# Every second column as the stationary operand: two feature tiles interleaved in each 256 columns of a weight unit

## The chip, the cores and the metric

The program runs on one core of a Trainium2 chip, batch 1, sequence 256, model width 1024. The metric is the device time of one execution in microseconds (us), as the median of several runs. Per-instruction times are in nanoseconds (ns).

## The reference

Two transformer blocks follow one another on the same 256 tokens. The first normalises its input, projects it with one wide matrix, runs two attention mixers (one with a learnt index that keeps the top 64 keys, one with compressed, selected and windowed keys), gates and adds their outputs, and ends in a squared-ReLU feed-forward layer. The second has a gated feed-forward layer, a mixer of dilated-window attention and an mLSTM, and a second gated feed-forward layer. What counts here is that nearly all of the work is products of the 256 tokens with float32 weight matrices:

```python
h = rmsnorm(x, norm_mix[l])
proj = h @ w_in[l]
...
x = x + jnp.square(jax.nn.relu(h @ w_mlp_in[l])) @ w_mlp_out[l]
...
f = swiglu(rmsnorm_2(x, ffn1_pre_g[l]), ffn1_w_gate[l], ffn1_w_up[l], ffn1_w_down[l])
x = x + 0.5 * rmsnorm_2(f, ffn1_post_g[l])
```

## The kernel before, in words

Every weight matrix is an object of class `Wt` (L40). It cuts the columns into chunks, mostly 512 wide (`widths`), and the rows into tiles of 128; a **unit** is two row tiles of one chunk, 128 x 1024 numbers, 512 KB. `layout` (L56) writes the units one after another into the array that the kernel receives; this happens on the host before the run and is outside the time. `plan` (L206) lists all 364 units in the order in which they are used.

For each unit `stream_dma` (L225) issues one DMA on SyncE's queue into a tile `raw`, and `stream_split` (L237) makes two tiles of it: ScalarE rounds `raw` to float32r as `hi` (L251), VectorE writes the remainder `lo = raw - hi` (L252). Both read and write whole rows, left to right. The activations are split in the same manner into `xh` and `xl`. A product then takes three matmuls: hi with xh, hi with xl, lo with xh. `load_unit` (L257) keeps splits two units ahead and DMAs five units ahead.

There are two ways to use a unit:

- `gemm_feat` (L322): the weights are the **stationary** operand. A block of 128 columns ("feature tile" f, four to a 512-wide chunk) is loaded into TensorE, and the 256 tokens stream past as the moving operand; the result has features on the partitions. For each row tile k and each f it issues the three matmuls L334, L336, L337, and each of them comes with its own weight load. Two feature tiles share one PSUM bank. 5,448 matmuls of the run are of this kind (1,816 on each line). All are 128 wide but 8 on each line, the 96 columns at the end of the first chunk of `W_IN1`.
- `gemm_tok` (L276): the tokens are stationary, two tiles of 128, and the weight columns stream past (L290 to L292), 512, 386 or 352 at a time.

Which chunk goes which way is written out in the code: the out- and down-projections (`W_OUT1`, `W_MO`, `W_D1`, `W_OUT2`, `W_D2`), chunk 4 of `W_IN1` and chunks 6 to 9 and 14 to 17 of `W_IN2` go through `gemm_tok`, everything else through `gemm_feat`.

TensorE's instructions stand in the order in which the program and its scheduler wrote them; smaller jobs (attention, transposes) are put in between by `flush` after each row tile. SyncE's and GpSimd's orders are those of the code.

The stationary operand is cut out of `hi` and `lo` like this:

```python
for f in range(nf):
    fs = slice(f * 128, min(f * 128 + 128, w))
    o = ps[f // 2][:fs.stop - fs.start, f % 2, :]
    nc.tensor.matmul(o, hi[:, fs], xh[:, k, :], start=(k == 0 and f % 2 == 0), stop=False,
                     skip_group_check=True)
```

Of the kernel before, what the change touches and what calls it, by code (L numbers as in the profile page):

```python
# [21 lines left out]
D = 1024  # L22
# [6 lines left out]
FF2 = 2816  # L29
VIF = 386  # L30
# [5 lines left out]
def widths_of(n):  # L36
    return [512] * (n // 512) + ([n % 512] if n % 512 else [])


class Wt:  # L40


    def __init__(self, name, k, widths):
        self.name, self.k, self.widths = name, k, widths
        self.kt = k // 128
        self.off, o = [], 0
        for w in widths:
            row = []
            for u in range(0, self.kt, KT):
                n = min(KT, self.kt - u)  # L50
                row.append((o, u, n))
                o += 128 * n * w
            self.off.append(row)
        self.size = o

    def layout(self, w):  # L56
        out = np.empty(self.size, w.dtype)
        c0 = 0
        for c, wd in enumerate(self.widths):
            for o, u, n in self.off[c]:  # L60
                blk = w[u * 128:(u + n) * 128, c0:c0 + wd].reshape(n, 128, wd).transpose(1, 0, 2)
                out[o:o + 128 * n * wd] = blk.reshape(-1)
            c0 += wd
        return out


def win1_columns():
    o = {}
    p = 0
    for n, w in (("q_a", 512), ("k_a", 64), ("v_a", 64), ("q_i", 256), ("k_i", 32), ("w_i", 8), ("q_b", 512),  # L70
                 ("kc", 128), ("vc", 128), ("ks", 128), ("vs", 128), ("kw", 128), ("vw", 128), ("g_b", 24),
                 ("g_br", 2048)):
        o[n] = np.arange(p, p + w)
        p += w
    qb = o["q_b"].reshape(2, 4, 64).transpose(1, 0, 2).reshape(-1)
    cols = [o["q_i"], o["k_a"], o["k_i"],
            o["kc"], o["vc"], o["ks"], o["kw"],
            o["q_a"], qb,
            o["v_a"], o["vs"], o["vw"], o["w_i"], o["g_b"],
            o["g_br"]]  # L80
    return np.concatenate(cols)


def win2_columns():
    o = {}
    p = 0
    for n, w in (("q", 1536), ("k", 1536), ("v", 1536), ("qk", 2048), ("v_m", 1024), ("o_m", 1024), ("if", 8),
                 ("g_a", 1024), ("g_m", 1024)):
        o[n] = np.arange(p, p + w)
        p += w  # L90
    cols = []
    for g in range(3):
        cols += [o["q"][g * 512:(g + 1) * 512], o["k"][g * 512:(g + 1) * 512]]
    cols += [o["v"], o["if"], o["qk"], o["v_m"], o["o_m"], o["g_a"], o["g_m"]]
    return np.concatenate(cols)


W_IN1 = Wt("w_in", D, [352] + [512] * 3 + [352] + [512] * 4)
W_BRA = Wt("w_branch_a", 512, [512] * 2)
W_BRB = Wt("w_branch_b", 512, [512] * 2)  # L100
W_OUT1 = Wt("w_out", D, [512] * 2)
W_MI = Wt("w_mlp_in", D, [512] * 8)
W_MO = Wt("w_mlp_out", 4096, [512] * 2)
FFW = widths_of(FF2)
W_G1 = Wt("ffn1_w_gate_2", D, FFW)
W_U1 = Wt("ffn1_w_up_2", D, FFW)
W_D1 = Wt("ffn1_w_down_2", FF2, [512] * 2)
W_IN2 = Wt("w_in_2", D, [512] * 6 + [VIF] * 4 + [512] * 12)
W_ATT = Wt("w_att_branch_2", 512, [512] * 2)
W_MLB = Wt("w_mlstm_branch_2", D, [512] * 2)  # L110
W_OUT2 = Wt("w_out_2", D, [512] * 2)
W_G2 = Wt("ffn2_w_gate_2", D, FFW)
W_U2 = Wt("ffn2_w_up_2", D, FFW)
W_D2 = Wt("ffn2_w_down_2", FF2, [512] * 2)
WEIGHTS = [W_IN1, W_BRA, W_BRB, W_OUT1, W_MI, W_MO, W_G1, W_U1, W_D1, W_IN2, W_ATT, W_MLB, W_OUT2, W_G2, W_U2, W_D2]

COL_GAINS = ["norm_mix", "norm_mlp", "norm_final", "ffn1_pre_g_2", "mix_pre_g_2", "ffn2_pre_g_2", "mlstm_head_g_2"]
# [47 lines left out]
def prep(inp):  # L165
    a = {}
    g = {k: np.asarray(v) for k, v in inp.items()}
    for w in WEIGHTS:
        m = g[w.name][0]
        if w is W_IN1:  # L170
            m = m[:, win1_columns()]
        elif w is W_IN2:
            m = m[:, win2_columns()]
# [23 lines left out]
class Prog:  # L197
# [8 lines left out]
    def plan(self):  # L206

        o = [(W_IN1, c) for c in (4, 0, 1, 3, 2, 5, 6, 7, 8)]
        for c in range(2):
            o += [(W_BRB, c), (W_BRA, c)]  # L210
        o += [(W_OUT1, 0), (W_OUT1, 1)]
        o += [(W_MI, c) for c in range(8)] + [(W_MO, 0), (W_MO, 1)]

        def ffn(g, u, d):
            r = []
            for c in range(len(FFW)):
                r += [(g, c), (u, c)]
            return r + [(d, 0), (d, 1)]
        o += ffn(W_G1, W_U1, W_D1)
        o += [(W_IN2, c) for c in (6, 0, 1, 2, 3, 4, 5, 7, 8, 9, 14, 15, 16, 17, 10, 18, 12, 19, 11, 13, 20, 21)]  # L220
        o += [(W_ATT, 0), (W_ATT, 1), (W_MLB, 0), (W_MLB, 1), (W_OUT2, 0), (W_OUT2, 1)]
        o += ffn(W_G2, W_U2, W_D2)
        return [(W, c, u) for W, c in o for u in range(len(W.off[c]))]
# [98 lines left out]
    def gemm_feat(self, W, c, xh, xl, done, rate=1, delay=0):  # L322

        nc = self.nc
        w = W.widths[c]
        nf = -(-w // 128)
        ps = [self.pacc.tile([128, 2, 256], F32, tag="acc", name="acc") for _ in range(-(-nf // 2))]
        for u in range(len(W.off[c])):
            for k, hi, lo in self.load_unit(W, c, u):
                last = k == W.kt - 1  # L330
                for f in range(nf):
                    fs = slice(f * 128, min(f * 128 + 128, w))
                    o = ps[f // 2][:fs.stop - fs.start, f % 2, :]
                    nc.tensor.matmul(o, hi[:, fs], xh[:, k, :], start=(k == 0 and f % 2 == 0), stop=False,  # L334
                                     skip_group_check=True)
                    nc.tensor.matmul(o, hi[:, fs], xl[:, k, :], start=False, stop=False, skip_group_check=True)  # L336
                    nc.tensor.matmul(o, lo[:, fs], xh[:, k, :], start=False, stop=last, skip_group_check=True)  # L337
                    if last and (f % 2 or f == nf - 1):
                        done(f // 2, ps[f // 2])
                if delay <= k < W.kt - 1:  # L340
                    self.flush(rate)
# [94 lines left out]
    def run(self):  # L436
# [5 lines left out]
        last = {W.name: i for i, (W, c, u) in enumerate(self.units)}  # L442
        ends = [last[W.name] + 1 for W in (W_D1, W_OUT2)]
        self.hold = [e + i for e in ends for i in range(2, 4)]
        self.ahead = {ends[0] + 1: 1}
        with ExitStack() as es:
# [36 lines left out]
            with self.banks(acc=6, tr=2):  # L483
                xf, xT, rs = self.mlp(x1)
                x = self.ffn(xf, xT, rs, W_G1, W_U1, W_D1, 1, "f1")
            self.dump("x3", x)
# [32 lines left out]
    def block1_mix(self, x0, x):  # L519
        tc, nc, ap, g = self.tc, self.nc, self.ap, self.g  # L520
        with ExitStack() as es, ExitStack() as rs_:
# [60 lines left out]
            def stats():  # L582
                s0 = self.small(2, "s0")
                with self.held(True):
                    for t in range(2):
                        self.ssq(s0[:, t:t + 1], x[:, t, :])
                v0 = self.small(2, "v0")
                self.mean_eps(v0, s0)
                self.newton_rsqrt(r0, v0, 2, "n0")
# [9 lines left out]
            stats()  # L599
            self.gemm_tok(W_IN1, 4, *xT, small_done, acc=self.psm)  # L600
            va = lambda s: tms[:, s, 0:64]
# [13 lines left out]
            self.later(rsB_job)  # L615
            self.gemm_feat(W_IN1, 0, *xT, d0)

# [50 lines left out]
            def d1(i, ps):  # L668
# [3 lines left out]
                for i, nm in enumerate("kv"):  # L672
# [12 lines left out]
                    blks.append(blk)  # L685
            self.gemm_feat(W_IN1, 1, *xT, d1)

# [274 lines left out]
            def odone(c):  # L962
                def f(t, ps):
                    cs = slice(c * 512, c * 512 + 512)
                    nc.vector.tensor_tensor(x[:, t, cs], ps, x[:, t, cs], op=ALU.add)
                return f
            for c in range(2):
                self.gemm_tok(W_OUT1, c, *mT, odone(c), delay=1, rate=2)
                self.later(*jx[4 * c:4 * c + 4])
# [4 lines left out]
    def mlp(self, x1):  # L974
# [11 lines left out]
        with tc.tile_pool(name="mlph", bufs=1) as hp, tc.tile_pool(name="mlpt", bufs=2) as tp:  # L986
# [22 lines left out]
            for c in range(2):  # L1009
                self.gemm_tok(W_MO, c, *hT, odone(c), delay=1, rate=2)  # L1010
                self.later(*jx[4 * c:4 * c + 4])
# [31 lines left out]
    def ffn2(self, x):  # L1043
# [15 lines left out]
        self.later(stats, self.narrow)  # L1059
        self.ffn(x, xT, rs, W_G2, W_U2, W_D2, 3, "f2", final=True)  # L1060

# [94 lines left out]
    def mixer2(self, x):  # L1156
        tc, nc, ap, g = self.tc, self.nc, self.ap, self.g
        xT, js = self.nextT
        with ExitStack() as es, ExitStack() as rs_:
# [119 lines left out]
            def g4(hs):  # L1279
                for h in hs:  # L1280
# [6 lines left out]
                                         scale=1.0)  # L1287
            self.gemm_tok(W_IN2, 6, *xT, vdone(0), head=2, mid=second, delay=3, rate=2)
            self.later(rsB_job)
            for c in range(6):  # L1290
                self.gemm_feat(W_IN2, c, *xT, qkdone(c % 2, c // 2))
            for c in range(1, 4):
                self.gemm_tok(W_IN2, 6 + c, *xT, vdone(c))
            self.flush()
# [227 lines left out]
            for c in range(2):  # L1522
                self.gemm_feat(W_MLB, c, *mlT, mdone(c), delay=1)
            return self.down_post(W_OUT2, mT, 2, x, 1.0, "m2", gcol=g["ffn2_pre_g_2"])

# [16 lines left out]
```

## Time and profile before

| | |
|---|---|
| runs | 1143.74, 1146.96, 1147.81 us; median 1146.96 us |
| the profiled execution | 1144.86 us, of which 1143.0 us from the first to the last instruction |
| TensorE matmul / weight load | busy 98% / 91% of the span |
| VectorE, ScalarE, GpSimd | 64%, 48%, 12% |
| mean granted TensorE clock | 0.991 of full speed |
| HBM | 192.84 MB read, 170 GB/s over the span |

"PE" is TensorE's matmul side and "PEld" its weight loads, which overlap the matmuls. A busy share says that some matmul was in flight; matmuls are pipelined, so one lasts longer than the distance from its start to the next start. How fast TensorE works is therefore read from the distance between starts, which this text calls the **pace**. A time's count "xN" joins N instructions in a row. L334 is line 334 of the kernel.

### The profile page before, as it was taken

Reading aid. Unit: us, or ns where it says so; the run is one execution under the profiler, and the core shown is the slowest. Engines: PE = TensorE matmul, PEld = TensorE weight load, DVE = VectorE, ACT = ScalarE, POOL = GpSimd, SP = SyncE. Lnnn points to the kernel's source line nnn. Section 1 sums busy time; section 2 is a strip of 40 time slices with the busy share of each in tenths; the row PEclk is TensorE's granted clock in tenths of the full one; section 3 lists DMA queues with packets and bytes.
Section 4 is the critical chain, followed back from the end, with each engine's and each line's share of the span. In section 5 each row is a group of like instructions: output and inputs, shape, how many; then the busy total and the mean of one; then the engine's idle time right before and its main releaser. Section 6 shows DMA issues by size and latency. Waiting matters only on the chain.

```text
span 1143.0 us, 19495 instructions
## 1 busy us (share of the span) xinstructions
PE 1117.7 (98%) x7808; PEld 1037.4 (91%) x7808; DVE 733.5 (64%) x1155; ACT 553.5 (48%) x818; POOL 136.9 (12%) x141
## 2 busy tenths in 40 slices
PE   8989999999999999999999998999999999999997
PEld 8888899899988899999888998889999988999986
DVE  6855776766654476656447686556779777656553
ACT  6324454455544455445446334545555556444442
POOL 1411230000000000000001775000323000000000
PEclk9998999999999999999999999999999999999999
DMA  8783114665555556655655664544545565665652
GB/s 295 252 189 102 57 56 148 198 186 188 184 184 188 183 191 195 186 176 177 211 173 168 199 186 148 165 130 148 177 147 164 165 190 173 189 188 159 211 190 80
DMA packets 57035, 197.03 MB, mean 172 GB/s; under 512 B 6828, under 2 KB 7100, under 8 KB 56688
## 3 DMA queue, kind: packets, MB, share of 16 engines
q1 hardware_dynamic: 53856, 186.44, 51.3%
q0 software_dynamic: 2800, 9.21, 3.3%
q8 instruction: 61, 1.00, 0.4%
q14 instruction: 30, 0.25, 0.1%
q10 hardware_dynamic: 288, 0.14, 0.0%
HBM read 192.84 MB, written 1.44 MB: 170 GB/s over the span
## 4 chain that ended last, share of the span: by engine, by line
PE 85%; POOL 5%; DMA 4%; DVE 3%; issue 1%; ACT 1%; DVEq 0%; SPq 0%; POOLq 0%; ACTq 0%
PE acc L334 16%; PE acc L336 16%; PE acc L337 16%; PE acc L292 9%; PE acc L291 9%; PE acc L290 9%; DMA sw<-qkT 2%; PE sm L801 2%; POOL sw L1221 2%; POOL qkT L1222 2%; PE o L834 1%; POOL qkT L1220 1%; DMA BT<-tvd 1%; DVE lo L252 1%; PE o L1343 1%
## 5 line engine op out<-in xcount | busy, mean ns | idle before, releaser
L252 DVE TENSOR_TENSOR lo<-raw,hi 128x1024 fp32r<-128x1024 f32 (+3 forms) x364 | 451.9, 1245 | 298.6 <-ACT hi L251 296.8
L251 ACT ACTIVATE hi<-raw 128x1024 fp32r<-128x1024 f32 (+3 forms) x364 | 373.1, 1026 | 447.9 <-PE acc L336 237.4
L334 PE MATMUL acc<-xh,hi 128*128 128x256 f32 x1656 | 467.7, 284 | 0.6 <-ACT hi L251 0.6
L336 PE MATMUL acc<-xl,hi 128*128 128x256 f32 x1656 | 467.4, 283 | 0.0
L337 PE MATMUL acc<-xh,lo 128*128 128x256 f32 x1656 | 466.3, 283 | 0.3 <-DVE lo L252 0.3
L334 PEld LDWEIGHTS acc<-xh,hi 128*128 128x128 f32 x1656 | 312.4, 189 | 4.4 <-issue 3.0
L336 PEld LDWEIGHTS acc<-xl,hi 128*128 128x128 f32 x1656 | 313.0, 189 | 2.4 <-issue 2.0
L337 PEld LDWEIGHTS acc<-xh,lo 128*128 128x128 f32 x1656 | 311.9, 189 | 1.9 <-issue 1.0
L292 PE MATMUL acc<-hi,hT 128*128 128x512 f32 x304 | 120.0, 395 | 0.0
L291 PE MATMUL acc<-lo,hT 128*128 128x512 f32 x304 | 119.7, 394 | 0.0
L290 PE MATMUL acc<-hi,hT 128*128 128x512 f32 x304 | 119.3, 395 | 0.0
L292 PEld LDWEIGHTS acc<-hi,hT 128*128 128x128 f32 x304 | 57.1, 188 | 13.5
L291 PEld LDWEIGHTS acc<-lo,hT 128*128 128x128 f32 x304 | 57.1, 188 | 13.3
L290 PEld LDWEIGHTS acc<-hi,hT 128*128 128x128 f32 x304 | 57.0, 188 | 13.0
L290 PE MATMUL acc<-hi,xh 128*128 128x386 f32 (+1 forms) x128 | 48.8, 382 | 0.9 <-ACT xh L368 0.9
L291 PE MATMUL acc<-lo,xh 128*128 128x386 f32 (+1 forms) x128 | 48.4, 378 | 0.0
L292 PE MATMUL acc<-hi,xl 128*128 128x386 f32 (+1 forms) x128 | 47.5, 377 | 0.2 <-DVE xl L369 0.2
L1040 POOL DMA_DIRECT2D row<-in_rows x4 | 2.3, 574 | 293.5 <-DVE xf L1023 214.6
L812 ACT ACTIVATE L<-L,nn 128x256 f32<-128x256 f32 (+1 forms) x48 | 21.2, 443 | 25.8 <-DVE nn L810 22.3
L290 PEld LDWEIGHTS acc<-hi,xh 128*128 128x128 f32 x128 | 24.3, 191 | 4.5 <-ACT xh L368 1.3
L292 PEld LDWEIGHTS acc<-hi,xl 128*128 128x128 f32 x128 | 24.4, 191 | 4.0 <-DVE xl L369 0.8
L291 PEld LDWEIGHTS acc<-lo,xh 128*128 128x128 f32 x128 | 24.6, 192 | 2.7 <-DVE lo L252 0.2
(414 smaller groups left out, 1261.3 us busy)
## 6 DMA issues: line engine op xcount, KB each, us to landing
raw<-in_w_in SPq DMA_DIRECT2D x100, 512.0 KB, 3.5
raw<-in_ffn_w_down SPq DMA_DIRECT2D x44, 512.0 KB, 4.2
raw<-in_ffn_w_gate SPq DMA_DIRECT2D x40, 512.0 KB, 3.6
raw<-in_ffn_w_up SPq DMA_DIRECT2D x40, 512.0 KB, 3.5
raw<-in_w_mlp_in SPq DMA_DIRECT2D x32, 512.0 KB, 4.0
raw<-in_w_mlp_out SPq DMA_DIRECT2D x32, 512.0 KB, 4.3
raw<-in_w_out SPq DMA_DIRECT2D x16, 512.0 KB, 3.5
raw<-in_w_in SPq DMA_DIRECT2D x16, 386.0 KB, 3.2
```

The source lines that it names most:

```text
L251: nc.scalar.activation(hi[:, :n * w], raw[:, :n * w], AF.Copy)
L252: nc.vector.tensor_tensor(lo[:, :n * w], raw[:, :n * w], hi[:, :n * w], op=ALU.subtract)
L290: nc.tensor.matmul(ps[t][:, :w], xh[:, k, sl], hi, start=(k == 0), stop=False)
L291: nc.tensor.matmul(ps[t][:, :w], xh[:, k, sl], lo, start=False, stop=False)
L292: nc.tensor.matmul(ps[t][:, :w], xl[:, k, sl], hi, start=False, stop=last)
L334: nc.tensor.matmul(o, hi[:, fs], xh[:, k, :], start=(k == 0 and f % 2 == 0), stop=False, skip_group_check=True)
L336: nc.tensor.matmul(o, hi[:, fs], xl[:, k, :], start=False, stop=False, skip_group_check=True)
L337: nc.tensor.matmul(o, lo[:, fs], xh[:, k, :], start=False, stop=last, skip_group_check=True)
L801: nc.tensor.matmul(ps[:, i, :], q[pr:pr + 64, U["fts"][i], t * 128:t * 128 + 128], kk, start=True, stop=True)
L812: nc.scalar.activation(L[:, i, :], L[:, i, :], AF.Exp, bias=nn[:, i:i + 1], scale=1.0, accum_out=lsum[:, t, br, h:h + 1])
L1221: nc.gpsimd.tensor_tensor(sw, sw, bc4(1), op=ALU.mult)
L1222: nc.gpsimd.tensor_tensor(q[0:32], q[0:32], sw, op=ALU.add)
```

## The change

In chunks that go through `gemm_feat`, the host now lays out each full 256 columns of a unit interleaved: column 0 of the first feature tile, column 0 of the second, column 1 of the first, and so on. `gemm_feat` undoes this when it cuts out the stationary operand: feature tile f takes every second column of its 256, starting at column f % 2. The remaining columns of a chunk (the 96 of the 352) stay contiguous. Chunks that go through `gemm_tok` keep the old layout; a new argument `tok` of `Wt` names them. The numbers that are multiplied, their order and the outputs are the same.

```diff
-    def __init__(self, name, k, widths):
-        self.name, self.k, self.widths = name, k, widths
+    def __init__(self, name, k, widths, tok=()):
+        self.name, self.k, self.widths, self.tok = name, k, widths, set(tok)
...
-                blk = w[u * 128:(u + n) * 128, c0:c0 + wd].reshape(n, 128, wd).transpose(1, 0, 2)
+                blk = w[u * 128:(u + n) * 128, c0:c0 + wd]
+                if c not in self.tok:
+                    p = wd // 256 * 256
+                    two = blk[:, :p].reshape(n * 128, p // 256, 2, 128).transpose(0, 1, 3, 2).reshape(n * 128, p)
+                    blk = np.concatenate([two, blk[:, p:]], 1)
+                blk = blk.reshape(n, 128, wd).transpose(1, 0, 2)
...
-W_IN1 = Wt("w_in", D, [352] + [512] * 3 + [352] + [512] * 4)
+W_IN1 = Wt("w_in", D, [352] + [512] * 3 + [352] + [512] * 4, [4])
...
-                    fs = slice(f * 128, min(f * 128 + 128, w))
-                    o = ps[f // 2][:fs.stop - fs.start, f % 2, :]
-                    nc.tensor.matmul(o, hi[:, fs], xh[:, k, :], start=(k == 0 and f % 2 == 0), stop=False,
+                    n = min(128, w - f * 128)
+                    if f // 2 < w // 256:
+                        part = lambda p: p[:, f // 2 * 256:f // 2 * 256 + 256].rearrange(
+                            "p (j h) -> p h j", h=2)[:, f % 2, :]
+                    else:
+                        part = lambda p: p[:, f * 128:f * 128 + n]
+                    o = ps[f // 2][:n, f % 2, :]
+                    nc.tensor.matmul(o, part(hi), xh[:, k, :], start=(k == 0 and f % 2 == 0), stop=False,
                                      skip_group_check=True)
-                    nc.tensor.matmul(o, hi[:, fs], xl[:, k, :], start=False, stop=False, skip_group_check=True)
-                    nc.tensor.matmul(o, lo[:, fs], xh[:, k, :], start=False, stop=last, skip_group_check=True)
+                    nc.tensor.matmul(o, part(hi), xl[:, k, :], start=False, stop=False, skip_group_check=True)
+                    nc.tensor.matmul(o, part(lo), xh[:, k, :], start=False, stop=last, skip_group_check=True)
```

## Rows read from the trace of the kernel before

**Rows 1.** The page's first part: busy time, share of the span and instruction count of each engine.

```profile
span 1143.0 us, 19495 instructions
PE 1117.7 (98%) x7808; PEld 1037.4 (91%) x7808; DVE 733.5 (64%) x1155; ACT 553.5 (48%) x818; POOL 136.9 (12%) x141
```

**Rows 2.** The chain of work that ended last: shares of the span by engine and by line, both from the page.

```profile
PE 85%; POOL 5%; DMA 4%; DVE 3%; issue 1%; ACT 1%; DVEq 0%; SPq 0%; POOLq 0%; ACTq 0%
PE acc L334 16%; PE acc L336 16%; PE acc L337 16%; PE acc L292 9%; PE acc L291 9%; PE acc L290 9%; DMA sw<-qkT 2%; PE sm L801 2%; POOL sw L1221 2%; POOL qkT L1222 2%; PE o L834 1%; POOL qkT L1220 1%; DMA BT<-tvd 1%; DVE lo L252 1%; PE o L13
```

**Rows 3.** TensorE's waits, whole span: who waited for whom, us in total, times, longest.

```profile
PE acc L334 <- ACT hi L251: 0.6, 2, 0.3
```

**Rows 4.** Timeline of PE in the squared-ReLU layer (`gemm_feat`): start us, duration us, line; the first and the last of 15 matmuls in a row, full clock.

```profile
299.77 0.28 PE L334 MATMUL acc<-xh,hi 128*128 128x256 f32 x1
...
301.42 0.28 PE L337 MATMUL acc<-xh,lo 128*128 128x256 f32 x1
```

**Rows 5.** The same view where the clock is halved (row of the windows view: stretch, us, PE busy and count, granted clock, DMA share, GB/s), and there the first and the last of 8 matmuls of `gemm_feat` in a row.

```profile
90.60:92.10 1.50, 1.50 (x9) 0.50 0.80 205
...
90.60 0.41 PE L337 MATMUL acc<-xh,lo 128*128 128x256 f32 x1
...
92.10 0.41 PE L334 MATMUL acc<-xh,hi 128*128 128x256 f32 x1
```

**Rows 6.** Timeline of PE in `gemm_tok`, 512 moving columns: the first and the last of 10 in a row, full clock.

```profile
349.70 0.39 PE L292 MATMUL acc<-hi,hT 128*128 128x512 f32 x1
...
351.79 0.40 PE L292 MATMUL acc<-hi,hT 128*128 128x512 f32 x1
```

**Rows 7.** Timeline of PE in the first chunk of `W_IN1`: three matmuls whose stationary operand has 96 columns, and the start of the next one.

```profile
22.92 0.28 PE L334 MATMUL acc<-xh,hi 128*96 128x256 f32 x1
23.04 0.28 PE L336 MATMUL acc<-xl,hi 128*96 128x256 f32 x1
23.16 0.28 PE L337 MATMUL acc<-xh,lo 128*96 128x256 f32 x1
23.27 0.28 PE L334 MATMUL acc<-xh,hi 128*128 128x256 f32 x1
```

**Rows 8.** Timeline of PEld around the compression layer: 16 loads of 128 columns in a row whose matmuls have only 30 moving columns (start us, us from the first start to the last end, count), and the start of the load behind them.

```profile
72.99 1.87 PEld L709 LDWEIGHTS sm<-blkv,w1v 128*128 128x128 f32 x16
74.79 0.19 PEld L334 LDWEIGHTS acc<-xh,hi 128*128 128x128 f32 x1
```

**Rows 9.** Weight loads grouped by line and shape: count, busy us, mean ns of one, idle time before.

```profile
L336 PEld LDWEIGHTS acc<-xl,hi 128*128 128x128 f32 x1648 | 311.8, 189 | 2.4 <-issue 2.0
...
L334 PEld LDWEIGHTS acc<-xh,hi 128*96 128x96 f32 x8 | 1.3, 161 | 0.0
```

**Rows 10.** GpSimd's groups by shape: an addition that reads contiguous rows (L791), and one that reads every sixteenth column (L682, two tiles).

```profile
L791 POOL TENSOR_TENSOR bm<-BT,M 128x512 f32<-128x512 f32 x6 | 8.6, 1440 | 0.0
...
L682 POOL TENSOR_TENSOR blkk<-kpk,csk 128x240 f32<-128x240 f32 x2 | 2.3, 1128 | 6.7 <-DMA kpk<-kv 6.7
L682 POOL TENSOR_TENSOR blkv<-kpv,csv 128x240 f32<-128x240 f32 x2 | 1.4, 743 | 2.4 <-DMA kpv<-kv 2.4
```

More of the change, by code (lines that the diff above doesn't have):

```diff
@@ L95, in win2_columns @@
     return np.concatenate(cols)
-W_IN1 = Wt("w_in", D, [352] + [512] * 3 + [352] + [512] * 4)
+W_IN1 = Wt("w_in", D, [352] + [512] * 3 + [352] + [512] * 4, [4])
 W_BRA = Wt("w_branch_a", 512, [512] * 2)
 W_BRB = Wt("w_branch_b", 512, [512] * 2)
-W_OUT1 = Wt("w_out", D, [512] * 2)
+W_OUT1 = Wt("w_out", D, [512] * 2, range(2))
 W_MI = Wt("w_mlp_in", D, [512] * 8)
-W_MO = Wt("w_mlp_out", 4096, [512] * 2)
+W_MO = Wt("w_mlp_out", 4096, [512] * 2, range(2))
 FFW = widths_of(FF2)
@@ L106 @@
 W_U1 = Wt("ffn1_w_up_2", D, FFW)
-W_D1 = Wt("ffn1_w_down_2", FF2, [512] * 2)
-W_IN2 = Wt("w_in_2", D, [512] * 6 + [VIF] * 4 + [512] * 12)
+W_D1 = Wt("ffn1_w_down_2", FF2, [512] * 2, range(2))
+W_IN2 = Wt("w_in_2", D, [512] * 6 + [VIF] * 4 + [512] * 12, [6, 7, 8, 9, 14, 15, 16, 17])
 W_ATT = Wt("w_att_branch_2", 512, [512] * 2)
 W_MLB = Wt("w_mlstm_branch_2", D, [512] * 2)
-W_OUT2 = Wt("w_out_2", D, [512] * 2)
+W_OUT2 = Wt("w_out_2", D, [512] * 2, range(2))
 W_G2 = Wt("ffn2_w_gate_2", D, FFW)
 W_U2 = Wt("ffn2_w_up_2", D, FFW)
-W_D2 = Wt("ffn2_w_down_2", FF2, [512] * 2)
+W_D2 = Wt("ffn2_w_down_2", FF2, [512] * 2, range(2))
 WEIGHTS = [W_IN1, W_BRA, W_BRB, W_OUT1, W_MI, W_MO, W_G1, W_U1, W_D1, W_IN2, W_ATT, W_MLB, W_OUT2, W_G2, W_U2, W_D2]
```

## The prediction, on record before the changed kernel ran

> **What bounds the kernel now.** I began with busy time by engine [rows 1]: TensorE has a matmul in flight for 98% of the span and a weight load for 91%, VectorE is next with 64%. A busy share alone proves nothing here, since matmuls overlap, so I went on to the chain of work that ended last [rows 2]. It runs through TensorE for 85% of the span, and the three lines of `gemm_feat`, the only ones whose operands the change touches, hold 3 x 16% = 48%, some 549 us. Then the waits [rows 3]: L334 waited for a weight split twice, 0.6 us in all. The matmuls of `gemm_feat` are thus not short of data; they run one behind the other, and the question is what sets their pace.
>
> The timeline gives that pace. At full clock 15 matmuls in a row start (301.42 - 299.77) / 14 = 117.9 ns apart [rows 4], each with its own weight load. Two things could set 117.9 ns: the 256 columns that stream past, or the load of the next 128 stationary columns. The rows say it is the stream. With half as many array cycles per time (granted clock 0.50) the pace is (92.10 - 90.60) / 7 = 214.3 ns [rows 5], nearly double. With 512 moving columns it is (351.79 - 349.70) / 9 = 232.2 ns [rows 6], nearly double, although there is still one load per matmul. And where the stationary operand has only 96 columns, so that its load shows 161 ns instead of 189 [rows 9], three matmuls still take (23.27 - 22.92) / 3 = 117 ns each [rows 7]: a shorter load buys nothing.
>
> But the load is close behind. Where the moving operand has just 30 columns, 16 loads of 128 float32 columns follow one another at (74.79 - 72.99) / 16 = 112.5 ns [rows 8]. That is the pace of the load by itself, read contiguously. The margin is 117.9 - 112.5 = 5.4 ns, under 5% of a load. This margin is the whole case: a longer load is free up to it, and beyond it each further nanosecond is paid by every matmul.
>
> **The change, part by part.** *The host's layout* lies outside the measured time. *DMAs*: the same number, sizes and order, nothing moves past any queue: 0 us. *The splits on ScalarE and VectorE* (L251, L252) read and write whole rows left to right as before, whatever column stands where: 0 us. *`gemm_tok`* keeps its layout and its instructions: 0 us. *PSUM and everything behind it*: f still names the same features in the same bank: 0 us. *Instructions*: as many matmuls and loads as before; no wait is added or taken away, so nothing new queues behind anything.
>
> What remains is the **address pattern of the weight loads**. Of the 5,448 matmuls of `gemm_feat` all but 3 x 8 (the 96-column ones) get a stationary operand with a step of 8 bytes instead of 4: 5,424 loads. Nothing in the trace shows such a load, so I bound it.
>
> - *Nothing*: the load keeps its 112.5 ns, stays under the 117.9 ns of the stream, and costs 0. What hides it is the matmul before it.
> - *The nearest rows with a stepped read* are GpSimd's, and they are far: another engine, and a step of 16 columns rather than 2 [rows 10]. Contiguous, 512 columns take 1440 ns, 2.81 ns a column; stepped, 240 columns take 743 and 1128 ns, 3.10 and 4.70 ns a column. The ratios are 1.10 and 1.67. On the load: 112.5 x 1.10 = 124 ns and 112.5 x 1.67 = 188 ns. The pace would rise by 124 - 118 = 6 ns or 188 - 118 = 70 ns, and the time by 5,424 x 6 = 33 us or 5,424 x 70 = 380 us. (The chain holds 549 us / 117.9 ns = 4,660 of them; the others stand beside GpSimd's and the DMAs' links and would come onto it as they grow, so this is the upper count.)
> - *Half the rate*, the far end: 225 ns, +107 ns, +581 us.
> - *Below nothing*: twice the pace at half the clock is a stream of 214.3 / 2 = 107.1 ns, so a full-clock matmul carries 117.9 - 107.1 = 10.8 ns more than its columns ask for; with 512 columns it is 232.2 - 214.3 = 17.9 ns. The growth, 7.1 ns for 256 columns, belongs to the stream; what is left, 10.8 - 7.1 = 3.7 ns a matmul, could belong to the load, since there is one of either. A load that reads elsewhere can at most win that: 5,424 x 3.7 = 20 us, or lose about as much.
>
> I take nothing, 0 us. GpSimd's rows speak of a step eight times as long; at the step of 2 half of what lies between the first and the last column is still used, and the better of the two stepped rows, 1.10, is almost inside the margin already.
>
> Here the Trainium skill weighs against GpSimd's rows. Its page "SBUF — State Buffer", section "Door 1: The DMA port swizzle", notes that SBUF is read in 16-byte lines, that two successive hits on a line are needed for full speed, and that each access which crosses to a new line pays. A step of 8 bytes still hits each line twice: by that rule the sum is 0 us, where the rows of GpSimd would make it 33 to 380 us; but it is the last step that is free. No row here shows it for TensorE.
>
> The sum: 1144.86 us of the profiled execution + 0 = 1144.9. That execution is 2.1 us below the median of the runs shown, so the forecast in terms of the median is 1147 us.
>
> **The rivals.**
>
> *The load becomes the bound* (slower). Place: every load of L334, L336, L337. It decides from a load of 117.9 ns, 5.4 ns or 4.8% over now; below it nothing is seen. For it: the margin is that thin, and every stepped row of the trace is dearer than the contiguous one. Against it: those rows are of another engine and of a step of 64 bytes. At 1.10 it gives 1147 + 33 = 1180 us, at 1.67 1527 us, at half the rate 1728 us. Chance 0.13 for up to 1180, 0.17 for more.
>
> The Trainium skill, page "TensorE: Matmul & The Clock Gate", section "LDWEIGHTS (loading the stationary operand)", gives a load as columns / 1.2, an estimate of 107 ns. The trace says 112.5 and decides; with 107 the point would lie at 10% instead of 4.8%, and the first of the three prices would vanish.
>
> *The two reads of TensorE meet less often* (faster). The stepped load walks its row at twice the pace, next to the moving stream. If the 3.7 ns come from the two reads meeting, up to 20 us go: 1127 us, and about 1137 if half of it goes. Against it: the shorter load of 96 columns did not shorten the pace by more than the rounding. Chance 0.15 for over 0.5%.
>
> *They meet more often* (slower): the same place, the other sign, up to 1147 + 20 = 1167 us. Chance 0.04.
>
> *The change does not do what it says*: the stepped operand could be issued as more than one load, or TensorE's program come out in another order. The number of instructions would show the first, the order of L334, L336, L337 the second. I see no ground for either; they are not given a price of their own.
>
> **How the numbers follow.** A measurement of this kernel can tell about 0.5%, 5.7 us, from no change; that is 1.05 ns a matmul over 5,424. Forecast, no change: 0.51. Faster 0.15. Slower 0.13 + 0.17 + 0.04 = 0.34. The likeliest single case is no change, 1147 us; its own range is 1141 to 1153. The 8-in-10 range reaches down to the faster rival's end, 1127, and up to the first price of the slower one, 1180; left out are the 0.17 of a load far beyond the margin. It is lopsided for that: the loss has no near ceiling, the gain has.
>
> **What would show it.** Right: the pace at full clock stays at 117 to 119 ns, the number of PE instructions at 7808, the chain's share of the three lines at 48%, and the load's own duration at 189 ns or less than 5 ns more. Wrong to the slow side: a pace above 119 ns on L334 to L337 and nowhere else, with the load's duration up by at least as much, the pace of `gemm_tok` still 232 ns, and VectorE and ScalarE idle for longer. Most telling would be the 96-column feature tile, which keeps its contiguous load: there the pace would stay at 117 ns while its neighbours slow down. Wrong to the fast side: a pace below 117 ns on the three lines with `gemm_tok` unchanged. If the time moved and the pace of the three lines did not, the whole account would be wrong.

## The result and the profile after

The changed kernel took 1153.71 us (median of 9 runs, 1149.55 to 1159.03) against 1145.81 us of the kernel before (9 runs on the same chip). The ratio is 1.0072, 95% interval 1.0049 to 1.0096: slower by 0.7%. A second series on another occasion (`after_again`, below) gave 1.0048, interval 1.0027 to 1.0070. The profiled execution below is the longest of its nine, 1159.03 us with a span of 1157.3 us; the paces that follow do not depend on that, since the second profile of the same kernel, with a span of 1148.1 us, has the same ones.

The page's first and fourth part after the change (L346, L348, L349 are the former L334, L336, L337; L297 to L299 the former L290 to L292):

```profile
span 1157.3 us, 19495 instructions
PE 1127.4 (97%) x7808; PEld 1046.8 (90%) x7808; DVE 734.6 (63%) x1155; ACT 554.4 (48%) x818; POOL 135.0 (12%) x141
...
PE 85%; POOL 5%; DMA 4%; DVE 3%; issue 1%; ACT 1%; DVEq 0%; SPq 0%; POOLq 0%; ACTq 0%
PE acc L346 16%; PE acc L348 16%; PE acc L349 16%; PE acc L297 9%; PE acc L299 9%; PE acc L298 9%; DMA BT<-tvd 2%; DMA sw<-qkT 2%; PE sm L813 2%; POOL sw L1233 2%; POOL qkT L1234 2%; PE o L846 1%; POOL qkT L1232 1%; DVE lo L259 1%; PE sm L1
```

As many instructions as in [rows 1], and the same shares of the chain as in [rows 2]. Nothing new waits. This span is 14.3 us longer than the one before, more than the paces below explain: TensorE's longest wait, one for a tile of VectorE (`gek`), happened to take 12.1 us here, against 7.1 before and 5.2 in the second profile. What changed is seen one level down, in the weight loads grouped by shape (count, busy us, mean ns of one) and in the timeline of the squared-ReLU layer:

```profile
L348 PEld LDWEIGHTS acc<-xl,hi 128*128 128x128 f32 x1648 | 323.8, 196 | 2.4 <-issue 2.0
```

```profile
301.80 0.29 PE L349 MATMUL acc<-xh,lo 128*128 128x256 f32 x1
...
305.90 0.29 PE L346 MATMUL acc<-xh,hi 128*128 128x256 f32 x1
```

A stepped load is shown with 196 ns where [rows 9] had 189. From the first of the two matmuls of the timeline to the second there are 34 distances between neighbouring starts, (305.90 - 301.80) / 34 = 120.6 ns, against 117.9 in [rows 4]. One stretch wanders by a nanosecond, so from here on a **mean pace** is the mean of all distances between the starts of neighbouring matmuls of `gemm_feat` in a trace at full clock, with distances over 140 ns left out. It was 118.21 ns before (some 5,180 distances, standard error 0.03) and is 119.75 ns after (as many, 0.04; 119.75 in the second profile too). In the kernels below whose stream changes its length from row tile to row tile, the first distance behind each change is left out as well: it is 65 ns in the mean in the kernels with half the stream and 114 to 133 ns at the lengths of the table further down, and belongs to neither of the two lengths. The difference, 1.54 ns, times 5,424 stepped loads is 8.4 us; times the 4,660 on the chain 7.2 us. The two measurements of the whole time gave 7.9 and 5.3 us.

Two controls stand in the same trace. The 96 columns of the first chunk kept their contiguous load:

```profile
22.67 0.28 PE L346 MATMUL acc<-xh,hi 128*96 128x256 f32 x1
22.79 0.28 PE L348 MATMUL acc<-xl,hi 128*96 128x256 f32 x1
22.90 0.28 PE L349 MATMUL acc<-xh,lo 128*96 128x256 f32 x1
23.02 0.29 PE L346 MATMUL acc<-xh,hi 128*128 128x256 f32 x1
```

(23.02 - 22.67) / 3 = 117 ns, as in [rows 7]. And `gemm_tok`, whose layout is the old one, keeps the pace of [rows 6]: (354.43 - 352.12) / 10 = 231 ns here, and over the whole trace 232.0 ns before and after.

```profile
352.12 0.40 PE L298 MATMUL acc<-lo,hT 128*128 128x512 f32 x1
...
354.43 0.40 PE L299 MATMUL acc<-hi,hT 128*128 128x512 f32 x1
```

So the loss sits in `gemm_feat`, and only where the load is stepped. What the result alone doesn't tell is whether the load became the slower of the two (L), whether it disturbs the stream that runs beside it (C), or whether each stepped load costs a fixed bit of issue (I).

### The profile page after: what moved, and what is told of

Read it like the earlier page. It is cut to its first block, busy times and chain, and to the rows that moved or that the text cites. A ratio compares the mean times of both kernels' runs of the same rounds, so it can differ in the third digit from the quotient of the medians.

```text
span 1157.3 us, 19495 instructions
## 1 busy us (share of the span) xinstructions
PE 1127.4 (97%) x7808; PEld 1046.8 (90%) x7808; DVE 734.6 (63%) x1155; ACT 554.4 (48%) x818; POOL 135.0 (12%) x141
## 4 chain that ended last, share of the span: by engine, by line
PE 85%; POOL 5%; DMA 4%; DVE 3%; issue 1%; ACT 1%; DVEq 0%; SPq 0%; POOLq 0%; ACTq 0%
PE acc L346 16%; PE acc L348 16%; PE acc L349 16%; PE acc L297 9%; PE acc L299 9%; PE acc L298 9%; DMA BT<-tvd 2%; DMA sw<-qkT 2%; PE sm L813 2%; POOL sw L1233 2%; POOL qkT L1234 2%; PE o L846 1%; POOL qkT L1232 1%; DVE lo L259 1%; PE sm L1325 1%
## 5 line engine op out<-in xcount | busy, mean ns | idle before, releaser
L259 DVE TENSOR_TENSOR lo<-raw,hi 128x1024 fp32r<-128x1024 f32 (+3 forms) x364 | 452.2, 1246 | 305.0 <-ACT hi L258 304.0
L346 PE MATMUL acc<-xh,hi 128*128 128x256 f32 x1656 | 471.0, 286 | 0.6 <-ACT hi L258 0.6
L348 PE MATMUL acc<-xl,hi 128*128 128x256 f32 x1656 | 470.3, 285 | 0.0
L349 PE MATMUL acc<-xh,lo 128*128 128x256 f32 x1656 | 469.3, 285 | 0.1
L346 PEld LDWEIGHTS acc<-xh,hi 128*128 128x128 f32 x1656 | 324.4, 196 | 4.5 <-issue 3.0
L348 PEld LDWEIGHTS acc<-xl,hi 128*128 128x128 f32 x1656 | 325.1, 196 | 2.4 <-issue 2.0
L349 PEld LDWEIGHTS acc<-xh,lo 128*128 128x128 f32 x1656 | 323.7, 196 | 1.6 <-issue 1.0
L299 PE MATMUL acc<-hi,hT 128*128 128x512 f32 x304 | 120.0, 395 | 0.0
L298 PE MATMUL acc<-lo,hT 128*128 128x512 f32 x304 | 119.7, 394 | 0.0
L297 PE MATMUL acc<-hi,hT 128*128 128x512 f32 x304 | 119.4, 395 | 0.0
L299 PEld LDWEIGHTS acc<-hi,hT 128*128 128x128 f32 x304 | 57.1, 188 | 13.5
L297 PEld LDWEIGHTS acc<-hi,hT 128*128 128x128 f32 x304 | 57.0, 188 | 13.0
L297 PE MATMUL acc<-hi,xh 128*128 128x386 f32 (+1 forms) x128 | 49.3, 387 | 0.9 <-ACT xh L380 0.9
L299 PE MATMUL acc<-hi,xl 128*128 128x386 f32 (+1 forms) x128 | 47.6, 378 | 0.2 <-DVE xl L381 0.2
L297 PEld LDWEIGHTS acc<-hi,xh 128*128 128x128 f32 x128 | 24.6, 193 | 4.6 <-ACT xh L380 1.3
L299 PEld LDWEIGHTS acc<-hi,xl 128*128 128x128 f32 x128 | 24.5, 192 | 4.0 <-DVE xl L381 0.8
```

Source lines behind the costliest of these rows:

```text
L259: nc.vector.tensor_tensor(lo[:, :n * w], raw[:, :n * w], hi[:, :n * w], op=ALU.subtract)
L297: nc.tensor.matmul(ps[t][:, :w], xh[:, k, sl], hi, start=(k == 0), stop=False)
L298: nc.tensor.matmul(ps[t][:, :w], xh[:, k, sl], lo, start=False, stop=False)
L299: nc.tensor.matmul(ps[t][:, :w], xl[:, k, sl], hi, start=False, stop=last)
L346: nc.tensor.matmul(o, part(hi), xh[:, k, :], start=(k == 0 and f % 2 == 0), stop=False, skip_group_check=True)
L348: nc.tensor.matmul(o, part(hi), xl[:, k, :], start=False, stop=False, skip_group_check=True)
```

## The experiments

### The load by itself: half the stream

The matmuls of `gemm_feat` stream 128 columns instead of 256, except in the first and last row tile of a chunk, once with the contiguous loads of before and once with the stepped ones.

```diff
+                    m = 256 if k == 0 or last else 128
-                    nc.tensor.matmul(o, part(hi), xh[:, k, :], ...
+                    nc.tensor.matmul(o[:, :m], part(hi), xh[:, k, :m], ...
...
```

> The kernel before, contiguous loads, but in gemm_feat all row tiles other than the first and the last of a chunk multiply only the first 128 of the 256 tokens, so the stream is half as long and the weight load has to show its own pace; the other tokens' sums are left incomplete. Theory L (the load is a pace of its own, 112.5 ns when contiguous, and the slower of load and stream decides): the short matmuls start 111 to 114 ns apart. Theory C (the load is far from the bound; a stepped load only disturbs the stream that runs beside it): the short matmuls start well under 110 ns apart, as a 128-column stream asks for 54 to 60 ns.

> The same half stream with the changed kernel's loads (every second column); the same sums are left incomplete. Theory L: the short matmuls start 119.5 ns apart (112.5 + the 7 ns by which the stepped load lasts longer in the changed kernel, 196 instead of 189), so 6 to 8 ns more than with contiguous loads, four times the difference of 1.5 ns that full-length matmuls show. Theory C: the difference to contiguous loads is 1.5 ns or less, since half the stream is there to be disturbed. Theory I (each stepped load costs a fixed 1.5 ns of issue, whatever runs beside it): 1.5 ns more than contiguous, 114 ns.

Timeline of PE in the squared-ReLU layer, 29 short matmuls with contiguous loads, then 27 with stepped ones:

```profile
267.82 0.28 PE L337 MATMUL acc<-xl,hi 128*128 128x128 f32 x1
...
270.95 0.28 PE L338 MATMUL acc<-xh,lo 128*128 128x128 f32 x1
```

```profile
267.83 0.28 PE L349 MATMUL acc<-xl,hi 128*128 128x128 f32 x1
...
270.90 0.28 PE L347 MATMUL acc<-xh,hi 128*128 128x128 f32 x1
```

(270.95 - 267.82) / 28 = 111.8 ns and (270.90 - 267.83) / 26 = 118.1 ns; the mean paces are 111.7 and 118.1 ns. Halving the stream hardly shortens the pace, so the load has a pace of its own close behind the stream's, and the step of 2 adds 6.4 ns to it, four times what full matmuls show. L holds, with 118.1 ns where it had 119.5; I, with 1.5 ns, falls. C's claim that the load is far from being the bound is refuted; whether a stepped load also disturbs the stream is taken up below.

### The step in two other places

`gemm_feat` as before; the tokens that are stationary in the out- and down-projections, and the weights of the compression layer, are read with a step of 2 (the host interleaves the latter, which the excerpt leaves out).

```diff
...
-            sl = slice(t * 128, t * 128 + 128)
+            sl = slice(t, 256, 2) if W in (W_OUT1, W_MO, W_D1, W_OUT2, W_D2) else slice(t * 128, t * 128 + 128)
...
-                    nc.tensor.matmul(ps[:, :30], cw[i][0][:, l, :], ...
+                    w1 = cw[i][0][:, l // 2 * 2:l // 2 * 2 + 2, :].rearrange("p a b -> p (a b)")
+                    nc.tensor.matmul(ps[:, :30], w1.rearrange("p (j h) -> p h j", h=2)[:, l % 2, :], ...
```

> The kernel before with a step of 2 in two other places: the tokens as stationary operand of the out- and down-projections (512 columns stream past; the results land in other token rows), and the weights of the compression layer (30 columns stream past; the host interleaves them, the sums stay the same). gemm_feat stays contiguous. Theory L: the 512-column pace stays 232.0 ns although each load lasts 7 ns longer (195 or 196 instead of 188), and the 16 loads of the compression layer go from 112.5 to 119.5 ns each; gemm_feat stays at 118.2 ns. Theory C: the 512-column pace rises by 1.5 to 3 ns and the compression layer's loads stay at 112.5. Theory I: both rise by 1.5 ns. The whole time moves by less than 0.3% by any of them.

The loads of the down-projections (grouped), and the timeline of PEld at the 16 loads of the compression layer:

```profile
L336 PEld LDWEIGHTS acc<-xl,hi 128*128 128x128 f32 x1648 | 311.7, 189 | 2.4 <-issue 2.0
...
L291 PEld LDWEIGHTS acc<-lo,hT 128*128 128x128 f32 x304 | 59.3, 195 | 11.1
```

```profile
73.31 1.97 PEld L710 LDWEIGHTS sm<-blkv,w1v 128*128 128x128 f32 x16
75.19 0.19 PEld L334 LDWEIGHTS acc<-xh,hi 128*128 128x128 f32 x1
```

The 16 loads, which have next to no stream beside them, take (75.19 - 73.31) / 16 = 117.5 ns each, against 112.5 in [rows 8]; the mean distance between the starts of these matmuls is 117.7 ns, against 111.6 before. In the down-projections a load shows 195 ns instead of 188, but the mean pace there is 232.3 ns instead of 232.0 (standard errors 0.1): 7 ns of load are hidden almost whole behind a stream of 512 columns. `gemm_feat` stays at 118.2 and the whole time at 1147.55 us (one run). L holds again, with a load 5 to 6 ns longer where it had 7; of C there may be 0.3 ns.

### Steps of 3, 4 and 8

Three, four or eight feature tiles are interleaved in a 512-wide chunk (at 8 the two row tiles of a unit share it), so that the stationary operand is every third, fourth or eighth column; with a step of 3 the fourth tile of each chunk stays contiguous. The operand for a step of 4, in place of the change's (the host's layout follows it):

```diff
...
-                        part = lambda p: p[:, f // 2 * 256:f // 2 * 256 + 256].rearrange(
-                            "p (j h) -> p h j", h=2)[:, f % 2, :]
+                        part = lambda p: p[:, f // 4 * 512:f // 4 * 512 + 512].rearrange(
+                            "p (j h) -> p h j", h=4)[:, f % 4, :]
```

> Four feature tiles interleaved in the 512 columns of a chunk, so that the stationary operand is every fourth column (chunks of 352 and 256 stay contiguous). If the price of a stepped load goes by the 16-byte lines it touches (32 contiguous, 64 at step 2: 7 ns for 32 more; 128 at step 4), the load takes 112.5 + 21 = 133.5 ns, the pace of gemm_feat is 133 to 134 ns and the time rises over the kernel before by some 5,000 x 15.5 ns = 75 us, to about 1221 us. If any step costs the same 7 ns, the pace is 119.7 ns and the time 1154 us. If two hits on a line are needed for full speed, as the Trainium skill says, a step of 4 has one hit and the load may go to half its rate: pace 200 to 225 ns, 1550 to 1680 us.

> In the 512-wide chunks three feature tiles are interleaved in 384 columns (step 3), the fourth stays contiguous. Step 2 gave a load its own pace of 117.4 ns with 64 lines of 16 bytes, step 4 gave 234 ns with 128 lines: both 1.83 ns a line. Theory N (a load takes 1.83 ns for every line it touches, and 111 ns at least): step 3 touches 96 lines, so the pace of three tiles in four is 176 ns, the fourth stays near 112 to 118, and the time is some 3,900 x 58 ns = 225 us over the kernel before, 1370 us. Theory H (less than two hits on every line halves the rate, as the note on lines reads): 234 ns for the three, about 1600 us.

> In the 512-wide chunks all eight feature tiles of a unit (two row tiles) are interleaved, so that the stationary operand is every eighth column. Theory N (lines touched): 128 lines as at step 4, so the same pace of 234 ns and the same time, 1743 us. Theory S (the price goes on growing with the distance): above 234 ns, up to 470 ns and 2900 us if it doubles again.

The loads grouped, step 4 and step 8:

```profile
L348 PEld LDWEIGHTS acc<-xl,hi 128*128 128x128 f32 x1648 | 533.6, 324 | 3.2 <-issue 2.9
```

```profile
L350 PEld LDWEIGHTS acc<-xl,hi 128*128 128x128 f32 x1648 | 545.3, 331 | 3.2 <-issue 2.9
```

The timeline at step 3: three matmuls of a contiguous tile from 300.39, then the next row tile's stepped ones from 300.74:

```profile
300.39 0.28 PE L345 MATMUL acc<-xh,hi 128*128 128x256 f32 x1
300.51 0.28 PE L347 MATMUL acc<-xl,hi 128*128 128x256 f32 x1
300.62 0.28 PE L348 MATMUL acc<-xh,lo 128*128 128x256 f32 x1
300.74 0.34 PE L345 MATMUL acc<-xh,hi 128*128 128x256 f32 x1
300.92 0.34 PE L347 MATMUL acc<-xl,hi 128*128 128x256 f32 x1
301.09 0.34 PE L348 MATMUL acc<-xh,lo 128*128 128x256 f32 x1
301.27 0.34 PE L345 MATMUL acc<-xh,hi 128*128 128x256 f32 x1
```

And the last three of 137 matmuls in a row at step 4:

```profile
308.58 0.40 PE L346 MATMUL acc<-oaT,hi 128*128 128x256 f32 x1
308.81 0.40 PE L348 MATMUL acc<-oaT,hi 128*128 128x256 f32 x1
309.05 0.40 PE L349 MATMUL acc<-oaT,lo 128*128 128x256 f32 x1
```

Step 4: (309.05 - 308.58) / 2 = 235 ns, in the median of the stepped matmuls too, and 1742.67 us against 1147.17 (ratio 1.5195, interval 1.5138 to 1.5251). My theory that the 7 ns would simply repeat for each further 32 lines (133 ns) was wrong; halving was the nearest of the three, although the pace and the time lie above its 200 to 225 ns and 1550 to 1680 us. That a load with less than two hits on a line goes at half its rate was my reading, in theory H too: the note in the Trainium skill, page "SBUF — State Buffer", section "Door 1: The DMA port swizzle", asks for two hits and gives no size for what is lost below them. Step 3: (301.27 - 300.74) / 3 = 177 ns, with 118 ns for the contiguous tile between, and 1362.28 us (one run) where 1370 was expected: not a threshold that halves the rate, but a price per line. Step 8: 241 ns in the median, 1778.31 us (one run): hardly more than step 4, although the load reaches twice as far. The 6 ns on top are not explained by the lines.

| step of the load | 16-byte lines touched | load's pace, ns | ns a line |
|---|---|---|---|
| 1 | 32 | 111.6 to 112.5 | (3.5) |
| 2 | 64 | 117.5 to 118.1 | 1.84 |
| 3 | 96 | 176 | 1.83 |
| 4 | 128 | 235 | 1.84 |
| 8 | 128 | 241 | 1.88 |

(Steps 1 and 2 beside short streams, the others as they stand in `gemm_feat`, where the stream of 118 ns is far shorter than the load.) A load thus costs about 1.84 ns for each line that it touches, or 112 ns, whichever is more. At step 2 the line price has just overtaken the other, by some 6 ns. The same note of the Trainium skill wants two hits on a line for full speed; the trace agrees nearly, since two hits cost 5% and fewer cost in proportion. Where the note goes on that float32 can stride by 4 for free, the trace disagrees: at a step of 4 the load takes 235 ns instead of 112, and the measurement decides.

### Which of the two is the bound at a step of 2: streams of other lengths

One kernel gives each row tile another length of the stream, with contiguous loads (where row tiles 1 and 2 also get a stepped stream), another does so with stepped loads.

```diff
+                    m = 256 if k == 0 or last else {1: 192, 2: 224, 3: 236, 4: 242, 5: 248, 6: 252}[k]
-                    nc.tensor.matmul(o, part(hi), xh[:, k, :], ...
+                    nc.tensor.matmul(o[:, :m], part(hi), xh[:, k, :m], ...
...
```

> The kernel before, contiguous loads, with a stream of another length in each row tile of gemm_feat: 128 columns at step 4 over two row tiles (row tile 1), 200 at step 2 (row tile 2), then 224, 236, 242, 248 contiguous columns (3 to 6), 256 in the others; the sums of gemm_feat are wrong or incomplete by that. Load alone: 111.1 ns. Stream alone at 118.2 / 256 = 0.462 ns a column: 103, 109, 112, 115 ns for 224 to 248. Theory M (two paces that are nearly equal add up to a little more than either, because each start waits for the later of the two): 111 to 112 at 224, then above both paces by 1 to 2 ns around 242 (113 to 114), 118.2 at 256. Theory C (only a stepped load disturbs): the larger of the two everywhere, 111, 111, 112, 115. The stepped streams: if a stream too pays 1.83 ns a line, 128 at step 4 takes 234 ns and 200 at step 2 takes 183 ns; if a stream pays by columns alone, both stay at 111 to 112.

> The changed kernel (every second column, load alone 117.4 ns) with streams of 192, 224, 236, 242, 248, 252 columns in row tiles 1 to 6 and 256 in the others; the sums of gemm_feat are incomplete by that. Stream alone: 89, 103, 109, 112, 115, 116 ns. Theory M: 117.4 ns up to 236, then creeping up to 119.7 at 256 as the two paces come together (118 at 242, 118.5 to 119 at 248 and 252). Theory C (the stepped load delays the stream by some 1.5 ns in 256 columns): 117.4 ns up to 252 columns, since a stream of 116 + 1.5 ns is hardly over the load, and then a step up to 119.7.

Mean paces, ns (470 to 525 distances each, some 1,190 at 256; standard errors 0.05 to 0.15):

| columns streamed | 224 | 236 | 242 | 248 | 252 | 256 |
|---|---|---|---|---|---|---|
| contiguous loads | 111.8 | 112.0 | 113.8 | 115.0 | | 118.3 |
| stepped loads | 118.4 | 118.5 | 119.1 | 119.2 | 118.9 | 119.7 |

Two row tiles with contiguous loads, from their second matmul to their last, 236 columns and then 242:

```profile
313.36 0.28 PE L340 MATMUL acc<-xl,hi 128*128 128x236 f32 x1
...
314.48 0.28 PE L341 MATMUL acc<-xh,lo 128*128 128x236 f32 x1
314.59 0.28 PE L338 MATMUL acc<-xh,hi 128*128 128x242 f32 x1
314.71 0.28 PE L340 MATMUL acc<-xl,hi 128*128 128x242 f32 x1
...
315.85 0.28 PE L341 MATMUL acc<-xh,lo 128*128 128x242 f32 x1
```

(314.48 - 313.36) / 10 = 112 ns and (315.85 - 314.71) / 10 = 114 ns. With contiguous loads the pace falls with the stream until, at 236 columns, it has reached the load's own pace. With stepped loads it falls by no more than 1.3 ns and ends at 118.4, again near the load's own pace of 118.1: a stream shorter by an eighth buys hardly anything. So a load takes about as long beside a long stream as beside a short one, and at a step of 2 it is level with the stream.

Where the two are level, the pace lies above both. A stream grows by (232.0 - 118.2) / 256 = 0.444 ns a column, so 242 columns should take 118.2 - 14 x 0.444 = 112.0 ns by themselves, which is an estimate. The contiguous load takes 111.7, and the pace is 113.8: 1.8 ns above either, with nothing stepped. Theory M had 113 to 114 ns there, theory C 112. With stepped loads, M's slow rise towards 256 columns is there too, though uneven, and it starts from 118.4 instead of 117.4 ns; C had no rise up to 252 columns. The changed kernel is the same case at 256 columns: 118.1 ns for the load, 118.2 for the stream, 119.7 for both. Why two level paces hold each other up is not shown. (192 columns are left out of the table; its row tile has gaps of other work in it.)

The stepped streams belong to another question, and surprised me; they stand in the last section.

### Which is the bound: narrower loads

The other way round: full streams, but a stationary operand of only 96, 112 or 120 columns in the row tiles between the first and the last.

```diff
+                    q = {1: 96, 2: 96, 3: 112, 4: 112, 5: 120, 6: 120}.get(k, n) if not last and n == 128 else n
-                    nc.tensor.matmul(o, part(hi), xh[:, k, :], ...
+                    nc.tensor.matmul(o[:q], part(hi)[:, :q], xh[:, k, :], ...
...
```

> The changed kernel (every second column), full streams of 256 columns, but the stationary operand has only 96 (row tiles 1, 2), 112 (3, 4) or 120 columns (5, 6) of a feature tile's 128 and all 128 in the others; the left-out features' sums are incomplete. A stepped load alone: 117.4 x 96/128 = 88 ns, 103 ns, 110 ns. Theory M (the start waits for the later of stream and load, and what was seen at 128 columns comes of two nearly equal paces): where the load is shorter than the stream the pace falls back to that of the kernel before, 118.2 ns at 96 and 112, at most 118.5 at 120, with 119.7 left at 128. Theory C (a stepped load in itself delays the stream beside it): 119.3 to 119.7 ns at all of them, as the steps are still there.

> The kernel before with the same narrower stationary operands, contiguous; the left-out features' sums are incomplete. Load alone: 83, 97, 104, 111 ns for 96 to 128 columns, all under the stream. Theory M: 118 ns at 128 and not more than 0.5 ns less at 96 to 120, so that the contiguous load takes hardly any part in the pace. If the load already has a share in 118.2 ns at 128 columns, the pace at 96 shows it as a fall of 1 ns or more.

| stationary columns | 96 | 112 | 120 | 128 |
|---|---|---|---|---|
| mean pace, stepped loads | 118.40 | 118.55 | 118.70 | 119.69 |
| mean pace, contiguous loads | 117.57 | 117.79 | 118.13 | 118.18 |
| difference | 0.83 | 0.76 | 0.57 | 1.51 |

(1,130 to 1,300 distances each, standard errors 0.06 to 0.1.) Shortening the stepped load does speed the pace up, by 1.0 ns from 128 to 120 columns and little more from there: below 120 columns the stream is the bound again. But it does not come back to the contiguous row. Some 0.6 to 0.8 ns stay although the load is far shorter than the stream. Its length is not the reason: by the estimates above a stepped load of 96 columns takes 88 ns and a contiguous one of 112 columns 97 ns, yet the former goes with 118.40 ns and the latter with 117.79. That part is C's: a stepped load beside the stream makes the stream itself a little slower.

So neither theory's forecast was met here: M had at most 118.5 ns up to 120 columns, C had 119.3 to 119.7 at all widths. Both effects are there. Beside a short stepped load the stream takes 118.4 ns, the stepped load by itself 118.1, and together they take 119.7, 1.3 ns above either. In the contiguous row the pace falls by 0.6 ns from 128 to 96 columns, where I had allowed 0.5: the load had a small part in the pace even before the change.

### The changed kernel again

> The changed kernel once more, for a second profile. Theories M and C alike: pace of gemm_feat 119.7 ns, load 196 ns, 512-column pace 232.0 ns, time 0.5 to 1% over the kernel before.

1152.07 us against 1146.8 us, ratio 1.0048 (1.0027 to 1.0070); mean pace 119.75 ns, 512-column pace 232.0. As expected in the paces; the time is just under the 0.5 to 1% that was expected.

## Why the prediction was right, and where it was not

*What sets the pace* was read rightly: the stream before the change, with the load close behind. Both halves of that are shown now, by shortening the one and the other: half the stream leaves 111.7 ns, three quarters of the load still 117.6.

*Everything that was costed at 0 but the loads* (DMAs, splits, `gemm_tok`, PSUM, instructions) stayed at 0: the count of instructions, the chain, the 512-column pace and the wait of L346 for `hi`, 0.6 us twice as in [rows 3], are those of before.

*The price of a stepped load* is the first of two steps that failed: "I take nothing, 0 us". The load does take longer, by 5 to 6.4 ns. That lies between the two values that I had bounded it by, 0 and the 1.10 of GpSimd's rows, which would have made 124 ns of 112.5; it was 117.5 to 118.1, a factor of 1.05. Weighing the rule of two hits against GpSimd's stepped rows was right in tendency, since it made a step of 2 the last free one, and steps 3 and 4 show how near the edge was. But nearly free is not free when the cover is 5%.

*The margin* is the second: "a longer load is free up to it", and the rival's "below it nothing is seen". The margin itself was about the right size: 118.2 ns less 111.6 to 112.5 is 6 to 7 ns, and the stepped load used nearly all of it. By the prediction's rule, that the slower of the two sets the pace, this load would still have cost next to nothing. What failed is that rule: with the load at 118.1 and the stream at 118.2 ns the pace is 119.7, and two level paces lie above either in the kernel without any step too. So the slower rival, "the load becomes the bound", is what came nearest, at a quarter of the price of its mildest case: 1.54 ns x 5,424 = 8.4 us instead of 33. Its list of signs was met: a pace above 119 on the three lines, the load's duration up by 7 ns, 232 ns in `gemm_tok`, 117 ns for the 96 columns, and a longer idle time of VectorE before L259, 305.0 us for 298.6. Two of the signs of being right, a pace of at most 119 ns and a load less than 5 ns longer, were not.

*The reads of TensorE meeting each other* I had as two rivals of opposite sign, at 3.7 ns a matmul at most. Of the losing one 0.6 to 0.8 ns are shown where the load is too short to be the bound; how much of the 1.5 ns at 128 columns is due to it and how much to the two paces being level cannot be told apart. Of the winning one nothing is shown. How the two reads delay each other is not shown either, only that they do.

*The range* held the time, and the forecast of no change was near, because the loss is small. That the stepped load ended level with the stream, and not 10 ns past it, stood in no term of the sum; that much was luck. The loss is just beyond what a measurement of this kernel can tell from nothing in the first series, and just under it in the second; "no change" was the likeliest case and "slower" what was measured, so the sign of the first series fell to the rival.

## What to carry to other kernels

Where a load and a stream run side by side, measure the pace of each by making the other short; a busy share tells nothing of how thin the cover is. A float32 stationary operand bears a step of 2 at about 5% of its load, and not much more: a step of 3 costs half as much again as one of 2, a step of 4 twice as much, a step of 8 hardly more than that. Two paces that are level do not give the slower of the two: here the pace came out 1.3 to 1.8 ns above both. A cost that is hidden by a few per cent of cover should therefore be forecast as a cost, not as zero.

## What the runs showed that was not expected

The stream is not priced like the load. In the kernel with contiguous loads and two stepped streams (128 columns at step 4, then 200 at step 2):

```profile
1005.95 0.30 PE L338 MATMUL acc<-xh,hi 128*128 128x128 f32 x1
...
1006.89 0.30 PE L341 MATMUL acc<-xh,lo 128*128 128x128 f32 x1
1007.01 0.37 PE L338 MATMUL acc<-xh,hi 128*128 128x200 f32 x1
...
1009.00 0.36 PE L341 MATMUL acc<-xh,lo 128*128 128x200 f32 x1
```

(1006.89 - 1005.95) / 8 = 117.5 ns for 128 columns at step 4 and (1009.00 - 1007.01) / 11 = 180.9 ns for 200 columns at step 2: 0.92 and 0.90 ns a column, twice the 118.2 / 256 = 0.46 ns of a contiguous stream, and the same for both steps. By the price of a line I had expected 234 and 183 ns, by columns alone 111 to 112 for both; the first of the two rules out the one, the second the other. A stream loses half its rate as soon as it is stepped and nothing more by step 4, while a load loses 5% at step 2 and half at step 4. So the tokens, which stream, must stay contiguous, where the weights, which are loaded, could just about afford a step.
